# A hybrid decoder layer: gates in seven half-size products, token sums on VectorE, two buffers for streamed weights

## The chip, the cores and the metric

The kernel runs on one core of one Trainium2 chip. Its time is the device time of one execution in microseconds; the median of three runs is given. PE is TensorE, DVE is VectorE, ACT is ScalarE, POOL is GpSimd, and SP is SyncE, which issues nearly all DMAs.

## The reference, cut to what matters

One layer with 4096 tokens of width 1024. Three head groups read the same normalised input `h`; the gate path is a part of the combined projection, SiLU of which multiplies the groups before the output projection.

```python
shift, scale, gate = jnp.split(c_act @ ada_w + ada_b, 3, axis=-1)
h = _rmsnorm(x, g_pre) * (1.0 + scale[:, None]) + shift[:, None]
proj = h @ w_in
aq, ak, av, ag, rkv, rg, gq, gkk, gv, gg = jnp.split(proj, list(np.cumsum(IN_SPLITS)[:-1]), axis=-1)
attn = _sliding_window_attention(...)
attn = attn * jax.nn.silu(ag)
...
rwkv = rwkv * jax.nn.silu(rg)
gla = _gla_mixer(h, gq, gkk, gv, gk1, gk2, gk_b, gla_norm_w) * jax.nn.silu(gg)
y = jnp.concatenate([attn, rwkv, gla], axis=-1) @ w_out
return x + gate[:, None] * _rmsnorm(y, g_post)
```

The gates `ag`, `rg` and `gg` together are a 1024 x 1024 product with `h`, as wide as the output projection.

## The kernel before, in words

Work goes in 16 steps of 256 tokens, in two halves. The first half (the block from line 644 on) computes `h`, transposed, as an f16 pair of high and low parts (`hT`: channel, 2 parts, 8 channel blocks, 256 tokens), and the RWKV and linear-attention groups, whose results go to HBM (`mscr`), as `hT` does (`hscr`). Beside it `stage_c` splits the weights of the second half into scaled f16 pairs and writes them to HBM (`wscr`, `woscr`). The second half does the attention projections (`qkv`, `heads_of`), the gates (`gates`, `gates_of`), the banded attention (`stage_s`, `attend`), the gating (`stage_m`) and the output projection with its norm (`outp`).

A product of two f16 pairs takes three matmuls (high by high, high by low, low by high). The gates are four column groups of 256 (`Wq[3]` to `Wq[6]`); `proj` makes each as two halves of 8 x 3 matmuls of 256 tokens, into one PSUM bank `gp`; ACT takes its tanh and DVE closes it (`ag`). The output projection is already in seven half-size products (Strassen's scheme in Winograd's form): `stage_m` builds sums of the gated blocks, `block` splits them into pairs (`mtp`), `outp` runs products `PRODUCTS`, each 12 matmuls of 512 columns into a bank `op`, and DVE adds the banks into `yv`. Four of its seven weight sets stay in SBUF (`o1`, `o6`, `o4`, `o5`), three are loaded anew in each step, in halves, into one buffer `ov`.

What sets the order: each engine's order is fixed beforehand by a planner, `Order.pin` (line 220), which simulates costs of its own and takes, of what is ready, the lowest rank: the place in the program less `order.urgent`. `URGENT` (line 36) lifts what frees a bank. Streams of stages (`streams`, `emit`) set the place in the program; `stage_p2` (line 1991) strings gates, projections and output of neighbouring steps together.

In the linear attention a 128 x 256 state `Gst` with a block-diagonal mask `bdm` is kept by one 128 x 256 f32 matmul `kvp` and three DVE operations per 128 tokens (`stage_r`, lines 1409 to 1417). Softmax rows are scaled by DVE (line 1756).

Of the kernel before, what the change touches and what calls it, by code (L numbers as in the profile page):

```python
# [35 lines left out]
URGENT = 150  # L36
# [362 lines left out]
def hybrid_kernel(ctx, tc, x, rows, ada1, adaw, w1, wl, w2, wo, cst, abias, out):  # L399
# [51 lines left out]
    wscr = dp.tile([7, P, 2, KD * 256], F16, name="wscr")  # L451
# [192 lines left out]
    with ExitStack() as p1:  # L644
# [233 lines left out]
        def wo_squares(h):  # L878

            for j in range(16 * h, 16 * h + 16):  # L880
                s32 = wt([P, 256], "cs", 2)
                SP.dma_start(s32, wo[:, j * 256 : (j + 1) * 256])
                yield [s32]
                S.activation(wt([P, 2, 256], "ch", 2, F16)[:, 0], s32, AF.Square, accum_out=wo_ss[:, j : j + 1])
            if h == 0:
                return
            sst = st.tile([P, 1], F32, tag="wss", name="wss")
            V.tensor_reduce(sst, wo_ss, axis=AX.X, op=ALU.add)
# [5 lines left out]
            pow2(wo_sc, w_inv[7], tot)  # L894

        def wo_group(k, c):


            left, right = [wt([P, 256], "cs", 2) for _ in range(2)]
            for t, k8 in ((left, k), (right, 4 + k)):  # L900
                for h in range(2):
                    col = c * P + h * 512
                    at = (col // 256) * 2048 + k8 * 256 + col % 256
                    SP.dma_start(t[:, h * P : (h + 1) * P], wo[:, at : at + P])
            w11, w12, w21, w22 = left[:, 0:P], left[:, P:], right[:, 0:P], right[:, P:]
            yield [left, right]

            def parts(t, p):
                m = t.shape[-1] // P
                t = t.rearrange("p (m c) -> p m c", m=m)  # L910
                z = wt([P, 2, 2, P], "ch", 2, F16)[:, 0:m]
                S.activation(z[:, :, 0, :], t, AF.Identity, scale=wo_sc)
                V.scalar_tensor_tensor(z[:, :, 1, :], t, wo_sc, z[:, :, 0, :], op0=ALU.mult, op1=ALU.subtract)
                SP.dma_start(woscr[p : p + m, :, k, c].rearrange("m p h c -> p m (h c)"), z.rearrange("p m h c -> p m (h c)"))

            parts(w11, 0)
            parts(right, 1)
# [3 lines left out]
            parts(left, 3)  # L921
# [3 lines left out]
            parts(right, 5)  # L925

        def stage_c(i):

            yield [("c", i - 1), ("vg", i)]
            for n in ((0,), (1, 2), (3,), (4, 5), (6,))[i] if i < 5 else ():  # L930
                src = w2[:, n * 2048 : (n + 1) * 2048]
                inv = w_inv[n]


                def piece(j):
                    s32 = wt([P, 256], "cs", 2)
                    SP.dma_start(s32, src[:, j * 256 : (j + 1) * 256])
                    return s32

                ss = st.tile([P, 2, KD], F32, tag="wss8", name="wss8")  # L940
                for j in range(KD):
                    s32 = piece(j)
                    yield [s32]
                    S.activation(wt([P, 2, 256], "ch", 2, F16)[:, 0], s32, AF.Square, accum_out=ss[:, 0, j : j + 1])
                    if n == 2:
                        S.activation(wt([P, 2, 256], "ch", 2, F16)[:, 0][:, 0:P], s32[:, 0:P], AF.Square, accum_out=ss[:, 1, j : j + 1])
# [3 lines left out]
                for o, iv, sx in parts:  # L950
                    sst = st.tile([P, 1], F32, tag="wss", name="wss")
                    V.tensor_reduce(sst, ss[:, o, :], axis=AX.X, op=ALU.add)
                    yield [sst, "mq"]
                    sp = mq("wssp")
                    PE.matmul(sp[:, 0:1], ones, sst, start=True, stop=True)
                    tot = st.tile([P, 1], F32, tag="wtot", name="wtot")
                    V.tensor_copy(tot, sp[:, 0:1])
                    pow2(sc if sx is None else sx, iv, tot)
                for j in range(KD):
                    s32 = piece(j)  # L960
                    yield [s32]
                    hi, lo = [t[:, n] for t in (wt([P, 2, 256], "ch", 2, F16),) for n in range(2)]
                    S.activation(hi, s32, AF.Identity, scale=sc)
                    V.scalar_tensor_tensor(lo, s32, sc, hi, op0=ALU.mult, op1=ALU.subtract)
                    SP.dma_start(wscr[n, :, 0, j * 256 : (j + 1) * 256], hi)
                    SP.dma_start(wscr[n, :, 1, j * 256 : (j + 1) * 256], lo)
# [12 lines left out]
                if n > 2:  # L979
                    V.tensor_single_scalar(g_h[n - 3], inv, 0.5, op=ALU.mult)  # L980
            if 4 <= i < 6:
                yield from wo_squares(i - 4)
            elif 6 <= i < NS - 2:
                for g in (i - 6, i + 2):
                    yield from wo_group(g % 4, g // 4)
# [392 lines left out]
        def stage_r(i):  # L1378
# [30 lines left out]
            for a in range(2):  # L1409
                gidx = 2 * i + a  # L1410
                Gc, Gn = Gst[gidx % 2], Gst[(gidx + 1) % 2]
# [17 lines left out]
                yield [Gn, "mq"]  # L1429
# [135 lines left out]
    def pool2(name):  # L1565
# [3 lines left out]
        "q", "kT", "vt", "w5", "w6", "ab", "v4", "pr", "mxa", "ag", "mtp", "mxb", "sm1", "o1", "o6", "o4", "o5", "ov")}  # L1569
# [8 lines left out]
    Wq = []  # L1578
# [48 lines left out]
    def qkv(i):  # L1627
# [12 lines left out]
        yield from heads_of(hT, q, kT, vt_, pjt, mq if i > 1 else pjt)  # L1640
# [592 lines left out]
```

## Time and profile before

| | us |
|---|---|
| median of 3 runs (2060.5 to 2067.3) | 2060.84 |
| the profiled execution's own time | 2064.53 |
| its span | 2062.4 |
| PE busy in the span | 1952.8 (95%) |
| DVE busy | 1608.5 (78%) |
| ACT busy | 1154.2 (56%) |
| POOL busy | 215.2 (10%) |

The span is from the first to the last instruction. Busy time counts an instruction from its start to its end; a matmul's end is modelled and overlaps the next, so two starts, not two durations, give its pace. A row names engine, operation, output and inputs; nearly all rows have line 334, that of the helper that records every operation, so they are told apart by the names of tiles.

### The profile page before, as it was taken

The numbers are of one execution on the slowest core, as the hardware profiler recorded it, in microseconds if no ns is written. First come the engines' busy times: TensorE is split into PE (matmuls) and PEld (weight loads), VectorE is DVE, ScalarE is ACT, GpSimd is POOL, SyncE is SP. The second block draws the span as 40 slices with busy tenths as digits, with TensorE's granted clock in tenths as the row PEclk, the third lists the DMA queues.
The fourth block names the chain that finished last, engine by engine and source line by source line (L and its number), as shares of the span: only waits on it lengthen the run. The fifth ranks groups of instructions, "written<-read, shape, count | busy, mean of one in ns | idle before, by whom it ended". The sixth has DMA issues, their size and how long they took to land.

```text
span 2062.4 us, 61554 instructions
## 1 busy us (share of the span) xinstructions
PE 1952.8 (95%) x24931; PEld 1515.7 (73%) x24931; DVE 1608.5 (78%) x5211; ACT 1154.2 (56%) x2765; POOL 215.2 (10%) x405
## 2 busy tenths in 40 slices
PE   5899999999999999999898999999999999999997
PEld 2678777787787877777777677777787777877783
DVE  5787888878877688996767887877778877778877
ACT  5867776576776856766334544443444444444543
POOL 1511111521111111111100000000000000000000
PEclk8999999999999999999999999999999999999999
DMA  9332233323322413345323434343334333333315
GB/s 366 109 100 75 80 102 105 87 92 110 92 88 82 129 37 98 114 128 181 108 73 134 162 108 144 117 134 100 124 114 147 106 126 116 115 124 130 123 45 175
DMA packets 182504, 242.11 MB, mean 117 GB/s; under 512 B 51650, under 2 KB 140226, under 8 KB 177988
## 3 DMA queue, kind: packets, MB, share of 16 engines
q1 hardware_dynamic: 182068, 237.57, 35.6%
q8 instruction: 198, 3.24, 0.7%
q14 instruction: 94, 0.77, 0.1%
q10 hardware_dynamic: 144, 0.52, 0.1%
HBM read 177.20 MB, written 60.82 MB: 115 GB/s over the span
## 4 chain that ended last, share of the span: by engine, by line
PE 57%; DVE 24%; DMA 8%; ACT 6%; issue 3%; SPq 2%; POOL 0%; DVEq 0%; ACTq 0%; POOLq 0%
PE gp L334 16%; PE op L334 12%; PE zz L334 5%; PE qp L334 3%; PE lp L334 3%; SPq L334 2%; PE sc L334 2%; DVE mtp L334 2%; PE ovp L334 2%; DVE q L334 2%; PE kp L334 2%; DVE pr L334 2%; PE gqk L334 2%; DMA cs<-in_wo 1%; DVE ch L334 1%
## 5 line engine op out<-in xcount | busy, mean ns | idle before, releaser
L334 PEld LDWEIGHTS <-mtp 128*128 128x128 f16 x1344 | 130.3, 98 | 141.0 <-issue 3.2
L334 PE MATMUL op<-o,mtp 128*128 128x512 f16 x768 | 172.3, 379 | 0.0
L334 ACT ACTIVATE pr<-pr,nm,lsc 128x256 f32<-128x256 f32 (+1 forms) x256 | 149.3, 585 | 33.8 <-DVE nm L334 33.7
L334 PE MATMUL op<-ov,mtp 128*128 128x512 f16 x576 | 143.1, 379 | 0.5 <-DVE q L334 0.5
L334 PEld LDWEIGHTS <-hT 128*128 128x128 f16 x1536 | 117.5, 99 | 26.0 <-issue 3.9
L334 DVE CUSTOM_DVE_ANT_0 pr<-sc,ab,kept 128x256 f32<-128x256 f32 (+1 forms) x256 | 108.6, 475 | 10.6 <-PE sc L334 10.4
L334 DVE TENSOR_TENSOR yv<-op,yv 128x512 f32<-128x512 f32 x105 | 70.3, 680 | 47.8 <-PE op L334 33.7
L334 PE MATMUL pv<-gvh,hT 128*128 128x272 f16 x512 | 98.8, 283 | 7.3 <-DVE kg L334 3.0
L334 ACT ACTIVATE ag<-gp,gh 128x512 f32<-128x512 f32 x64 | 43.7, 683 | 109.5 <-PE gp L334 109.5
L334 POOL COPY kT<-kT 128x512 f16<-128x512 f16 x15 | 10.1, 676 | 844.4 <-DVE kT L334 815.3
L334 ACT ACTIVATE mtp<-yv,oi 128x1024 f16<-128x1024 f32 x30 | 34.3, 1143 | 111.7 <-DVE yv L334 111.3
L334 PE MATMUL lp<-hT,Lh 128*128 128x256 f16 x512 | 93.5, 276 | 0.1
L334 DVE SCALAR_TENSOR_TENSOR ag<-ag,gp 128x512 f32<-128x512 f32 x64 | 43.7, 683 | 59.7 <-ACT ag L334 59.7
L334 PE MATMUL zz<-hT,vh 128*128 128x256 f16 x512 | 88.8, 273 | 1.3 <-DVE zb L334 1.3
L334 PE MATMUL zz<-hT,rh 128*128 128x256 f16 x512 | 89.9, 275 | 0.0
L334 PE MATMUL zz<-hT,kh 128*128 128x256 f16 x512 | 89.8, 273 | 0.0
L334 PE MATMUL gqk<-hT,gqkh 128*128 128x256 f16 x512 | 89.8, 276 | 0.0
L334 PE MATMUL gp<-hT,q5h 128*128 128x256 f16 x512 | 87.0, 273 | 1.4 <-DVE ag L334 1.4
L334 PE MATMUL gp<-hT,q3h 128*128 128x256 f16 x512 | 86.0, 273 | 1.9 <-DVE yv L334 1.4
L334 PE MATMUL qp<-hT,q1h 128*128 128x256 f16 x512 | 86.0, 273 | 0.6 <-DVE kT L334 0.6
L334 PE MATMUL qp<-hT,q0h 128*128 128x256 f16 x512 | 85.2, 273 | 1.1 <-DVE nwt L334 1.1
L334 PE MATMUL gp<-hT,q6h 128*128 128x256 f16 x512 | 85.5, 273 | 0.0
(460 smaller groups left out, 6034.9 us busy)
## 6 DMA issues: line engine op xcount, KB each, us to landing
ov<-woscr SPq DMA_DIRECT2D x96, 512.0 KB, 3.8
xt<-in_x SPq DMA_DIRECT2D x16, 1024.0 KB, 5.1
hscr<-hT SPq DMA_DIRECT2D x16, 1024.0 KB, 5.3
hT<-hscr SPq DMA_DIRECT2D x16, 1024.0 KB, 5.2
x<-in_x SPq DMA_DIRECT2D x30, 512.0 KB, 4.2
out<-yv SPq DMA_DIRECT2D x30, 512.0 KB, 2.9
cs<-in_w SPq DMA_DIRECT2D x112, 128.0 KB, 2.4
v<-vscr SPq DMA_DIRECT2D x128, 64.0 KB, 2.3
```

The source lines that it names most:

```text
L334: r = f(*args, **kw)
```

## The change

The gates become seven half-size products, too. `h` is cut in four quarters (128 tokens by 512 channels), `sums` builds four combinations of them on DVE, with ACT's casts for their high parts (`sg`, in step 0 `mtp`), and a product runs 4 x 4 x 3 matmuls of 128 tokens; DVE and ACT combine the banks into `ag`. The weights are combined in the first half (`group`, for gates and output alike, in pieces of 512 columns) and lie in `gwscr`. Four of seven gate sets stay in SBUF (`g`). Gates and output share two buffers for streamed sets (`ov`, `ov2`), which `feed` fills two sets ahead, in halves; of the output's sets one more (5) is streamed. Sets 0 of the last gates and the last two outputs have room of their own.

Besides: `heads_of` takes the gates between keys and values, and values go before the queries; the scaling of softmax rows goes to ACT; the reciprocal root of single columns needs fewer operations; `URGENT` is 600 and covers the blocks and their scale; the linear-attention state is kept packed, 128 x 64.

```diff
-URGENT = 150
+URGENT = 600
...
+        if n == 1:
+            for c in (3.0, 12.0, 768.0):
+                V.scalar_tensor_tensor(tt[:, :n], y, y, v, op0=ALU.mult, op1=ALU.mult)
+                V.scalar_tensor_tensor(y, tt[:, :n], -c, y, op0=ALU.add, op1=ALU.mult)
+            V.tensor_single_scalar(y, y, -1.0 / 8192, op=ALU.mult)
+            return
...
-                if gidx > 0:
-                    V.tensor_scalar(Gc, Gc, egm[:, a, 0:1], None, op0=ALU.mult)
+                V.scalar_tensor_tensor(heads4[0], now.rearrange("p (o n) -> p o n", o=1).to_broadcast([P, 4, HD]),
+                                       egm[:, a, 0:1], heads4[1], op0=ALU.mult, op1=ALU.mult)
                 kvp = mq("kvp")
-                PE.matmul(kvp[:, :NT], kt[:, a, :], vg[:, a, 0:256], start=True, stop=True)
-                V.tensor_tensor(Gn, kvp[:, :NT], Gc, op=ALU.add)
-                V.scalar_tensor_tensor(Gn, Gn, egp[:, a, 128:129], bdm, op0=ALU.mult, op1=ALU.mult)
+                joint()
+                for h in range(4):
+                    PE.matmul(kvp[32 * h : 32 * h + 32, 0:HD], kt[:, a, 32 * h : 32 * h + 32], vg[:, a, h * HD : h * HD + HD],
+                              start=True, stop=True)
+                joint(False)
+                V.scalar_tensor_tensor(then, now, egm[:, a, 0:1], kvp[:, 0:HD], op0=ALU.mult, op1=ALU.add)
+                V.tensor_scalar(then, then, egp[:, a, 128:129], None, op0=ALU.mult)
...
+    PRODUCTS = ((0, False), (1, True), (6, True), (3, False), (4, True), (5, False), (2, False))
+    GATES = ((1, True), (0, False), (6, True), (4, False), (3, True), (5, True), (2, False))
...
+    def feed(h):
+
+        if fed[h] < len(feeds):
+            src, n = feeds[fed[h]]
+            SP.dma_start(Wv[fed[h] % 2][:, 2 * h : 2 * h + 2], src[n, :, 2 * h : 2 * h + 2])
+            fed[h] += 1
...
+        whole(X, 1, 0)
+        whole(Y, 1, 1)
+        later()
+        V.tensor_tensor(Y, X, Y, op=ALU.add)
+        parts(Y, 0)
+        whole(Z, 0, 0)
+        later()
+        V.tensor_tensor(Y, Y, Z, op=ALU.subtract)
+        parts(Y, 1)
+        later()
+        V.tensor_tensor(X, Z, X, op=ALU.subtract)
+        parts(X, 2)
+        whole(Z, 0, 1)
+        later()
+        V.tensor_tensor(Z, Z, Y, op=ALU.subtract)
+        parts(Z, 3)
...
+        moving = (a12, a11, s2, s3, s1, a22, s4)
...
+            for c in range(4):
+                for k in range(KD // 2):
+                    for a, b in ((0, 0), (0, 1), (1, 0)):
+                        PE.matmul(po[:, c], W[c // 2][:, c % 2, k, a, :], moving[n][b][:, k, :],
+                                  start=k == a == b == 0, stop=k == KD // 2 - 1 and a == 1)
+                    if c % 2 and k == KD // 2 - 1 and not stays and W is not own:
+                        after(c // 2)
...
+        def close(to, j, z, t):
+            for m in range(2):
+                S.activation(t[:, 2 * m : 2 * m + 2], z[:, 2 * m : 2 * m + 2], AF.Tanh, scale=g_h[2 * j + m])
+            V.scalar_tensor_tensor(to, t, 1.0, z, op0=ALU.add, op1=ALU.mult)
...
+        yield from full(0)
+        soon(S.copy, Y, banks[0])
+        yield from full(1)
+        soon(V.tensor_tensor, g11, banks[1], Y, op=ALU.add)
+        soon(S.copy, X, banks[1])
+        yield from full(2)
+        soon(V.tensor_tensor, g12, banks[2], X, op=ALU.add)
+        close(g11, 0, g11, Y)
+        yield from full(3)
+        soon(V.tensor_tensor, g22, banks[3], g12, op=ALU.add)
+        yield from full(4)
+        soon(S.copy, X, banks[4])
+        V.tensor_tensor(g12, g12, X, op=ALU.add)
+        V.tensor_tensor(Z, g22, X, op=ALU.add)
+        yield from full(5)
+        soon(V.tensor_tensor, g21, banks[5], g22, op=ALU.add)
+        close(g22, 1, Z, X)
+        close(g21, 0, g21, Y)
+        yield from full(6)
+        soon(V.tensor_tensor, g12, banks[6], g12, op=ALU.add)
+        close(g12, 1, g12, Z)
...
-            V.tensor_scalar(pr[h // 4][:, h % 4, k0:], pr[h // 4][:, h % 4, k0:], rd[:, h : h + 1], None, op0=ALU.mult)
+            S.activation(pr[h // 4][:, h % 4, k0:], pr[h // 4][:, h % 4, k0:], AF.Identity, scale=rd[:, h : h + 1])
...
+        elif 1 < i < NS - 1:
+            if i < NS - 2:
+                yield from outp(i - 1)
+            yield from stage_u(i)
+            yield from qkv(i + 1, gates(i))
```

In `sums`, `whole` adds the two parts of a quarter on DVE, and `parts` casts a sum on ACT and subtracts on DVE.

The planner's order moves in three places. On PE, at the border of two gate products in the middle of the second half (`q3` and `q4` are column groups of the weights before, `g` and `ov` weight sets now, h and l their parts), before:

```order
L334 LDWEIGHTS q4h
L334 MATMUL gp<-hT,q4h 128x256
L334 LDWEIGHTS q4l
L334 MATMUL gp<-hT,q4l 128x256
L334 LDWEIGHTS q4h
```

and in the change:

```order
L334 MATMUL gp<-hT,g_18592 128x128
L334 LDWEIGHTS ov
L334 MATMUL gp<-hT,ov 128x128
L334 MATMUL ovp<-pr,v_21067 64x128 x14
L334 MATMUL ovp<-pr,v_22070 64x128 x2
```

A gate matmul has half the tokens, and every one still comes with a weight load of its own; products on streamed weights (`ov`) stand between those on weights that stay.

On DVE, where the scale of the gated values (`mtot` to `msc`) leads to the first block of the output product (`mtp`), before:

```order
L334 TENSOR_REDUCE mtot<-mp 128x1
L334 TENSOR_SCALAR p2e<-mtot 128x1
L334 TENSOR_SCALAR p2e<-p2e 128x1 x2
L334 TENSOR_SCALAR p2f<-p2e 128x1
L334 TENSOR_SCALAR p2e<-p2e 128x1
L334 TENSOR_SCALAR msc<-p2f 128x1
L334 TENSOR_SCALAR miv<-p2e 128x1
L334 TENSOR_TENSOR oi<-miv,winv_98 128x1
L334 SCALAR_TENSOR_TENSOR mtp<-mxa,msc,mtp 128x512
```

and in the change (`xg` and `sg` are the token sums, `q` the queries):

```order
L334 TENSOR_REDUCE mtot<-mp 128x1
L334 TENSOR_TENSOR xg_18559<-xg_18561,xg_18559 128x512
L334 TENSOR_SCALAR p2e<-mtot 128x1
L334 TENSOR_TENSOR xg_18561<-hT 128x512
L334 TENSOR_SCALAR p2e<-p2e 128x1
L334 TENSOR_TENSOR sg_18555<-xg_18560,sg_18555 128x512
L334 SCALAR_TENSOR_TENSOR q<-qp,q 64x512
L334 TENSOR_SCALAR p2e<-p2e 128x1
L334 TENSOR_TENSOR sg_18556<-xg_18559,sg_18556 128x512
L334 SCALAR_TENSOR_TENSOR q<-qp,q 64x512
L334 TENSOR_SCALAR p2f<-p2e 128x1
L334 TENSOR_SCALAR p2e<-p2e 128x1
```

One more sum (`xg`) follows before `msc`; what stood in a row is now drawn apart by five sums and two operations on the queries.

On SP, the DMAs of a step of the second half from the next tokens (`hT`) on (`vscr` and `v` spread the values, `mxb` the first half's results), before:

```order
L334 DMA hT<-hscr 128x4096
L334 DMA vscr<-vt 128x2x128
L334 DMA ov<-woscr 128x2048
L334 DMA v_24516<-vscr 32x4x128 x4
L334 DMA v_24517<-vscr 32x4x128 x4
L334 DMA ov<-woscr 128x2048 x3
L334 DMA mxb<-mscr 128x1024
L334 DMA ov<-woscr 128x2048 x2
L334 DMA out<-yv 128x1024
```

and in the change:

```order
L334 DMA hT<-hscr 128x4096
L334 DMA ov<-woscr 128x2048 x2
L334 DMA vscr<-vt 128x2x128
L334 DMA v_25082<-vscr 32x4x128 x4
L334 DMA v_25083<-vscr 32x4x128 x4
L334 DMA ov_18553<-woscr 128x2048 x2
L334 DMA mxb<-mscr 128x1024
L334 DMA ov<-woscr 128x2048 x2
L334 DMA ov_18553<-gwscr 128x2048 x2
L334 DMA ov<-gwscr 128x2048 x2
L334 DMA ov_18553<-gwscr 128x2048 x2
L334 DMA out<-yv 128x1024
```

Between the next tokens and the output six sets now stand, where three stood; they come from two places and go to two buffers in turn, one set of them ahead of the values.

## Rows read from the trace of the kernel before

**Rows 1.** Stages (windows): us, busy of PE, PEld, DVE, ACT, POOL, PE clock, DMA share, GB/s.

```profile
400.00:500.00 100.00, 97.80 (x1429) 79.46 (x1427) 79.82 (x320) 74.44 (x177) 17.26 (x38) 1.00 0.38 114
...
1000.00:1120.00 120.00, 103.08 (x1633) 82.86 (x1631) 79.39 (x295) 48.06 (x124) 8.18 (x15) 0.96 0.29 91
...
1364.46:1426.95 62.49, 61.60 (x639) 46.89 (x638) 48.89 (x136) 27.97 (x71) 0.61 (x1) 1.00 0.37 121
```

**Rows 2.** Page part 4, the chain that ended last, shares by engine.

```profile
PE 57%; DVE 24%; DMA 8%; ACT 6%; issue 3%; SPq 2%; POOL 0%; DVEq 0%; ACTq 0%; POOLq 0%
```

**Rows 3.** Timeline of PE in one step: start, duration (us), idle before.

```profile
1373.37 5.34 PE L334 MATMUL op<-o,mtp 128*128 128x512 f16 x24
...
1415.41 0.28 PE L334 MATMUL mp<-mss,first 128*128 128x2 f32 x2
...
1422.70 1.89 PE L334 MATMUL op<-ov,mtp 128*128 128x512 f16 x8
...
1425.48 0.60 PE L334 MATMUL sc<-kT,q 128*128 128x256 f16 x4 [0.89 <-DVE m L334]
```

**Rows 4.** Costliest groups of that step, PE: busy us, mean ns, idle before.

```profile
L334 PE MATMUL gp<-hT,q5h 128*128 128x256 f16 x32 | 5.5, 273 | 0.0
...
L334 PE MATMUL gp<-hT,q4l 128*128 128x256 f16 x16 | 4.4, 273 | 0.0
```

**Rows 5.** Timeline of PE, the 48 matmuls of one gate's column group.

```profile
1201.29 0.38 PE L334 MATMUL gp<-hT,q4h 128*128 128x256 f16 x2
...
1206.53 0.38 PE L334 MATMUL gp<-hT,q5h 128*128 128x256 f16 x2
```

**Rows 6.** Timeline of PE's weight loads, the value projection.

```profile
1481.53 2.77 PEld L334 LDWEIGHTS <-hT 128*128 128x128 f16 x48
...
1484.26 0.81 PEld L334 LDWEIGHTS <-q 128*128 128x128 f16 x8
```

**Rows 7.** Groups of that step, DVE.

```profile
L334 DVE TENSOR_TENSOR yv<-op,yv 128x512 f32<-128x512 f32 x7 | 4.7, 680 | 3.4 <-PE op L334 2.3 <-issue 1.2
...
L334 DVE TENSOR_SCALAR pr<-pr,rd 128x256 f32<-128x256 f32 x16 | 4.5, 348 | 0.1
...
L334 DVE SCALAR_TENSOR_TENSOR q<-qp,q 64x512 f16<-64x512 f32 x4 | 2.8, 688 | 1.9 <-ACT q L334 1.9
...
L334 DVE SCALAR_TENSOR_TENSOR ag<-ag,gp 128x512 f32<-128x512 f32 x4 | 2.7, 686 | 4.4 <-ACT ag L334 4.4
```

**Rows 8.** Timeline of DVE in that step.

```profile
1376.26 1.25 DVE L334 TENSOR_TENSOR yv<-op,yv 128x512 f32<-128x512 f32 x2
...
1377.43 1.22 DVE L334 STREAM_TRANSPOSE pr<-pr 128x1024 f32<-128x1024 f32 x1
...
1416.66 0.16 DVE L334 TENSOR_REDUCE mtot<-mp 128x1 f32<-128x2 f32 x1
...
1418.67 0.75 DVE L334 SCALAR_TENSOR_TENSOR mtp<-mxa,msc,mtp 128x512 f16<-128x512 f32 x1 [0.53 <-ACT mtp L334]
```

**Rows 9.** Groups of that step, ACT.

```profile
L334 ACT ACTIVATE vt<-vp,winv 128x256 f32<-128x256 f32 x1 | 0.5, 473 | 0.0
```

**Rows 10.** DMA of that step: GB/s in slices, packets, issues (KB each, us to landing).

```profile
GB/s 198 143 321 5 0 52 281 278 60 10 194 170 296 178 189 58 320 294 0 0 10 0 0 160 286 226 0 147 393 142 0 0 0 0 0 10 0 0 110 316
...
DMA packets 3144, 7.57 MB, mean 121 GB/s; under 512 B 337, under 2 KB 1598, under 8 KB 3009
...
ov<-woscr SPq DMA_DIRECT2D x6, 512.0 KB, 3.8
```

**Rows 11.** Timeline of PE, the linear-attention state in the first half.

```profile
113.27 0.60 PE L334 MATMUL kvp<-vg,kt 128*128 128x256 f32 x2
...
113.80 0.65 PE L334 MATMUL op<-Gst,qg 128*64 128x256 f32 x4
```

**Rows 12.** Groups of the whole span by form, DVE, splits of output weights.

```profile
L334 DVE SCALAR_TENSOR_TENSOR ch<-cs,wsc,ch 128x256 f16<-128x256 f32 x56 | 29.8, 539 | 6.5 <-ACT ch L334 5.9 <-DMA adr<-AT 0.3
```

**Rows 13.** Page part 5, costliest groups, weight loads of tokens.

```profile
L334 PEld LDWEIGHTS <-hT 128*128 128x128 f16 x1536 | 117.5, 99 | 26.0 <-issue 3.9
```

More of the change, by code (lines that the diff above doesn't have):

```diff
@@ L900, in wo_group, with group @@
+        def group(gate, k, c):
+            src, base, sc = (w2, 3, g_sc[c]) if gate else (wo, 0, wo_sc)
+            left, right = [wt([P, 512], "cs", 2).rearrange("p (h n) -> p h n", h=2) for _ in range(2)]
             for t, k8 in ((left, k), (right, 4 + k)):
                 for h in range(2):
[L902 to L905, printed above, removed]
+                    at = (base + c + 2 * h) * 2048 + k8 * 256
+                    SP.dma_start(t[:, h], src[:, at : at + 256])
+            w11, w12, w21, w22 = left[:, 0], left[:, 1], right[:, 0], right[:, 1]
@@ L918, in wo_group @@
+            if gate:
+                for t in (w12, w22):
+                    V.tensor_scalar(t, t, g_r[c], None, op0=ALU.mult)
+            parts(w11, 0, 1)
+            parts(right, 1, 2)
             V.tensor_tensor(w11, w12, w11, op=ALU.subtract)
@@ L950, in stage_c @@
                 for o, iv, sx in parts:
[L951 to L960, printed above, removed]
-                    yield [s32]
[L962 to L966, printed above, removed]
+                    yield from total(ss[:, o, :], sc if sx is None else sx, iv)
+                for j in range(4):
+                    s32 = piece(w2, n * 2048 + j * 512)
+                    yield [s32]
+                    z = split_tile().rearrange("p c h n -> p (c h n)").rearrange("p (h n) -> p h n", h=2)
+                    S.activation(z[:, 0], s32, AF.Identity, scale=sc)
+                    V.scalar_tensor_tensor(z[:, 1], s32, sc, z[:, 0], op0=ALU.mult, op1=ALU.subtract)
+                    SP.dma_start(wscr[n, :, :, j * 512 : (j + 1) * 512], z)
                 if n == 2:
@@ L978, in stage_c @@
                 V.tensor_scalar(inv, inv, hinv, None, op0=ALU.mult)
[L979 to L985, printed above, removed]
+            if 3 <= i < 5:
+                for n in (i, i + 2):
+                    yield from gate_squares(n)
+            elif 5 <= i < 7:
+                yield from wo_squares(i - 5)
+            for _ in range((0, 0, 0, 0, 1, 1, 1, 2, 2, 2, 2, 2, 2, 1, 0, 0)[i]):
+                yield from group(*next(groups))
         def stage_g(_):
@@ L1658, in heads_of @@
         model.order.urgent = 0
+        if mid is not None:
+            yield from mid
+        yield ["pj"]
+        vp = pj("vp")
+        for a in range(2):
+            yield from proj_tok(vp[:, a * P : (a + 1) * P], Wq[2], P, P, hT, a * P)
+        model.order.urgent = URGENT
+        S.activation(vt_.rearrange("p a n -> p (a n)"), vp[:, :NT], AF.Identity, scale=Wq[2][2])
+        model.order.urgent = 0
+        spread()
         for n in range(2):
-            yield ["pj"]
-            qp = pj("qp")
+            yield ["m" if n and pv is mq else "pj"]
+            qp = mt("qp") if n and pv is mq else pj("qp")
             for b in range(2):
@@ L1670, in heads_of @@
             model.order.urgent = 0
-        yield ["mq" if pv is mq else "pj"]
-        vp = pv("vp")
-        for a in range(2):
-            yield from proj_tok(vp[:, a * P : (a + 1) * P], Wq[2], P, P, hT, a * P)
-        model.order.urgent = URGENT
-        S.activation(vt_.rearrange("p a n -> p (a n)"), vp[:, :NT], AF.Identity, scale=Wq[2][2])
-        model.order.urgent = 0
     def spread_values(vt_, v4, i):
@@ L1686, in gates, with stage_u @@
+    def stage_u(i):
+        load_h(i)
+        yield [F[i]["hT"]]
+        F[i]["S"] = blocks if i == 0 else sums_t
+        sums(F[i]["hT"], F[i]["S"])
     def gates(i):
-        yield [("og", i - 2)]
+        yield [("og", i - 1)] if i > 1 else []
         f = F[i]
-        f["ag"] = ag = t_A([P, 8, NT], "ag") if i == 0 else pools["ag"].tile([P, 8, NT], F32, name="ag2") if i == 1 else F[i - 2]["ag"]
-        yield from gates_of(f["hT"], ag, pjt)
+        f["ag"] = t_A([P, 8, NT], "ag") if i < 2 else F[1]["ag"]
+        yield from gates_of(f["hT"], f["S"], f["ag"], feed, own=Wx.get(("g", i)))
@@ L1714, in stage_s, with home, attend @@
         vblk = [F[i - 1]["v"][1] if i > 0 else None, *v4]
[L1715 removed]
+        def home():
+            if "mx" not in f:
+                f["mx"] = wt([P, 4, NT], "mxa", 2)
+            return f["mx"]
         for a in range(2):
[L1717 to L1719 removed]
+            yield from attend(q, kT, vblk, home, a, i == 0 and a == 0, sct=sct, ovt=ovt, gate=[("o", i - 2)])
+    def attend(q, kT, vblk, home, a, first, before=None, sct=("at", "sq"), ovt=("tr", "m", "y", "mq"), gate=()):
         k0 = P if first else 0
@@ L2031, in hybrid_kernel @@
     xo, gn = x2[:, 0, :], x2[:, 1, :]
-    mtp = pools["mtp"].tile([P, 4, 2, 4, P], F16, name="mtp")
-    blocks, split = [mtp[:, n] for n in range(4)], []
     streams((0, "v", stage_v, None), *((1, "s", stage_s, i) for i in range(1, NS)), *((2, "m", stage_m, i) for i in range(NS)),
```

283 lines of the change are left out of this document (184 added, 99 removed).

## The prediction

> **What bounds the kernel now.** I read the stages first, then the chain of waits, then the groups of one step. The stage view gives two neighbouring parts of the second half and one of the first [rows 1]: a 256-token step takes 62.49 us, in which PE is busy 61.60, DVE 48.89 and ACT 27.97; the granted clock is 1.00, the upper of its two levels. The chain that ended last lies on PE for 57% of the span and on DVE for 24% [rows 2]; with PE at 61.60 of 62.49, a step of the second half ends when PE has worked through its matmuls. Of its waits one is worth a name: 0.89 us for a score bank that DVE frees [rows 3]. In the first half PE is busy 97.80 of 100 us and DVE 79.82; where the halves meet, PE idles 17 us of 120 [rows 1]. So two questions decide: what the gates cost PE after the change, and whether DVE, which pays for them, still hides.
>
> **Gates on PE.** A step's gates are now 4 x (32 + 16) = 192 matmuls of 256 columns [rows 4]. 48 of them start over 1206.53 - 1201.29 = 5.24 us [rows 5], 0.1092 us each, 20.97 us a step. The change makes 7 products x 4 x 4 x 3 = 336 matmuls of 128 columns, each still with its own weight load. The same shape is in the trace: the value projection's 48 loads, one before each 128-column matmul, take 1484.26 - 1481.53 = 2.73 us [rows 6], 0.0569 us each. So 336 x 0.0569 = 19.12, and 1.85 us a step come back; 16 x 1.85 = 29.6 us. Seven products for eight would give 2.6 a step, but half as wide a matmul costs 0.52, not 0.50, of a full one. Break-even is 20.97 / 336 = 0.0624 us a matmul.
>
> Here a page speaks against the change. The Trainium skill, "TensorE: Matmul & The Clock Gate", section "Back-to-back issue gap", says that in real streams of load and matmul a 128-column matmul takes about 81 ns, a 512-column one about 131. By that the new gates would cost 336 x 0.081 = 27.2 us a step and the kernel would lose some 100 us. This trace agrees with neither figure: 57 ns for the first, and 24 of the second take 5.34 us [rows 3], over 216 each. I keep the row.
>
> **VectorE.** Removed a step: 16 scalings of the softmax, 4.5 us [rows 7], which go to ACT, and four tiny steps of the shorter root, at the 0.16 of such a row [rows 8] 0.6 us. The four closing multiplies of a gate stay four. Added: 12 operations of 512 columns for the token sums (of hi and lo halves into f32, their combinations, the new low halves) and 7 that combine products. One costs 0.585 where two follow each other (1377.43 - 1376.26, [rows 8]) and 0.680 as a group [rows 7]; 19 make 11.1 to 13.0. Net +6.0 to +7.9: DVE is busy 54.9 to 56.8 of about 61 us, 90 to 93%. It hides behind PE as long as it fills the waits that it has today, where its next instruction waits for ACT or PE: 4.4 us before the gates' multiplies, 3.4 before the output sums, 1.9 before q [rows 7]. The sums are ranked below everything, and the order puts them between other operations.
>
> That has a price at one place, the second order excerpt. The step's scale goes through seven small DVE operations, and the first output product waits for it. Now mp starts at 1415.41 and the product at 1422.70 [rows 3], 7.29 us later; the scale's first operation starts at 1416.66 and the block is done at 1418.67 + 0.75 = 1419.42 [rows 8], 3.3 us early. In the change five sums stand between those seven, 5 x 0.585 = 2.9, and on PE 54 or 60 projection matmuls and 8 score matmuls follow mp, 6.8 to 7.4 us at 0.1092. The block comes at 4.0 + 2.9 = 6.9: between 0.5 early and 0.1 late, with nothing left for a wait on ACT in the two q rows between. Bounds: 0, and 1.0 (a q row with its share of the 1.9 wait). I take 0.4 a step, 6.4 us in all, nearer to the lower end, since only some of the chain's waits can fall there. Behind the block nothing else is late: the next ones have a product of 2.6 us each.
>
> **ScalarE.** 16 scalings at the 0.473 of a 256-column row [rows 9], four casts for the new hi halves and three bank copies at twice that, and eight tanh halves of 256 columns add at most 7.6 + 6.6 + 3.8 = 18.0: 46 of 61 us. Cost nothing; if DVE waits for it, that is the 0.4 above.
>
> **Weights and SP's queue.** Streamed sets go from 3 to 7 a step, 6 to 14 halves of 512 KB [rows 10]. The step moves 7.57 + 4.2 = 11.8 MB, 193 GB/s over 61 us; single slices of today's step show 393 [rows 10]. With two buffers the shortest return is one buffer's: out product 5 to gate product 0, with out product 2 and gate product 1 between, 2.6 + 2.7 = 5.3 us, and as much again as half a product, 1.3, for each half. A half lands in 3.8 us. Today's shortest, out 3 to out 2, is 5.2 and shows no wait worth naming. The third excerpt shows what is queued: the scattered v loads and the next hT stand behind loads that wait for PE, as before. Cost nothing; if the cover goes, see the rivals.
>
> **The first half.** The linear-attention state becomes a quarter as wide. Its kvp matmul holds PE for 113.80 - 113.27 = 0.53 us [rows 11], 32 times, 17 us. The new one, four of 32 x 64 side by side, saves at most all of that and at worst nothing; two changes of the array's tiling are against it, and PE is not free to use all of it. I take a quarter, 4 us. DVE's three state operations get narrower. The preparation of the weights handles 512 columns at a time, and gates are split in seven parts like the output weights: where 56 splits of 0.539 us [rows 12] stood, 12 and 32 wider ones stand with 32 more adds, about as much in all. DVE has 20 us of 100 free there, so it costs nothing; the bound is 8 us either way, about a third of what PE idles there at 2.2 us in 100 [rows 1]. Where the halves meet, 24 sums (14 us of DVE, which has 40 of 120 free) come before the first gates; again nothing, at half of PE's idle time, 8 us, either way. At the end the last gates save their 1.85 like the others, and the last output blocks are unchanged.
>
> **The sum.** -29.6 + 6.4 - 4 = -27.2. The profiled execution took 2064.53 us, 3.7 over the median of the three runs, 2060.84; it would take 2037.3, and the runs 2033.6. I forecast 2034. Its own range: late blocks 0 to 16, kvp 0 to -17, and twice 8 either way that hardly add up in full: 2016 to 2049.
>
> **Rivals.** *DVE sets the pace.* For it: 54.9 to 56.8 busy, and an in-order engine whose waits for ACT between two halves of a bank (kT and q) no order of work removes; the 13.6 us that it idles today would have to shrink to 4 to 6. If 6 us of its waits stay, a step takes 56.8 + 6 = 62.8, 0.3 over now; 16 x 0.3 - 4 gives +1, and with the sums filling part of them 0.2 to 0.5 less a step: about 2057. Against it: the sums depend only on hT, which is there a step earlier. 18%.
>
> *The weight stream is late*: the slower one. Place: the two returns of 5.2 and 5.3 us. In 5.2 us around out product 5 four halves, 2.1 MB, are asked for, 400 GB/s, above the highest slice of 393. A half has 6.5 us; up to there nothing is lost. At a landing of 9 us each return is 2.5 late, 5.0 a step, 14 steps 70 us, less 27: 2104. It decides from about 7.2 us on, where two returns cost the 1.45 that a step gains. Against it: 3.8 us today, at 37% of the DMA engines' time in a step [rows 1]. 7%.
>
> *The narrow matmul does not keep 0.0569.* A weight load by itself takes 99 ns [rows 13]. If in the gates it no longer ran beside the matmul before it, 336 x 0.099 = 33.3 us, +12.3 a step: about 2260. The Trainium skill's 81 ns, named above, is the milder form of this. Against it stands the value projection, 48 loads in 2.73 us in the midst of the same step. 3%.
>
> **How the numbers follow.** The forecast's case has 72%. A measurement of this kernel tells 0.5% from no change, 10.3 us, so faster begins at 2050.5. Of the 72, 64 lie below that; of the first rival's 18, 3 are faster, 13 the same, 2 slower; the other 10 are slower. Faster 0.67, same 0.21, slower 0.12. The range takes the forecast's own and reaches up to the first rival: 2014 to 2059, which leaves out the last two rivals and the ends.
>
> **What would show it.** Right: a step of 60.5 to 61.5 us, gate matmuls of 128 columns starting every 57 ns, DVE at 90% or more in a step and not first on the chain, ACT near 40 us. The first out product after mp shows an idle of some tenths released by DVE mtp. Wrong: out or gp matmuls on ov that wait for a DMA (second rival); PE idle of over 1.5 us a step released by DVE at several places (first); a pitch over 62 ns in gp (third). The first half would be at odds with me if its end moved by over 10 us.

## The result, and the profile after

The change takes 2072.66 us (median of 20 runs, 2064.35 to 2076.13) where the kernel before takes 2065.59 (20 runs, among them the three ahead of the prediction, which had 2060.84). The ratio is 1.0036, 95% interval 1.0026 to 1.0046: 7.4 us slower, clear of noise but under the 0.5% that the prediction counts as a change, where 2034 was forecast. The profiled execution took 2073.81 us, its span 2072.0, 9.6 us over the span before.

First the stages again, now of the change, with columns as in [rows 1]: one stretch of the first half and two steps of the second.

```profile
400.00:500.00 100.00, 91.74 (x1465) 74.81 (x1464) 91.68 (x318) 68.68 (x150) 29.90 (x46) 0.97 0.37 111
...
1422.82:1486.16 63.34, 61.31 (x790) 47.52 (x789) 54.57 (x134) 39.62 (x98) 1.04 (x1) 1.00 0.55 186
1486.16:1548.75 62.59, 59.74 (x778) 46.12 (x776) 54.94 (x134) 39.60 (x98) 1.04 (x1) 1.00 0.56 188
```

A step takes 62.97 us on the mean of these two, 0.5 more than before. PE is busy 60.5 (1.1 less than before), so it now idles 2.4 us a step, not 0.9. DVE is busy 54.8, the lower end of the forecast. In the stretch of the first half that is shown PE falls from 97.80 to 91.74 where DVE rises from 79.82 to 91.68.

To see where the difference lies, both traces are split at the first scale, the start of the first `mtot`. It comes at 1117.35 us before and at 1127.02 in the change, 9.7 us later; what follows, before and then in the change, is equally long:

```profile
1117.35:2062.38 945.03, 918.02 (x9403) 688.76 (x9401) 742.73 (x2053) 425.17 (x1074) 11.41 (x15) 1.00 0.37 122
```

```profile
1127.02:2072.03 945.01, 897.47 (x11448) 684.82 (x11445) 821.21 (x2022) 592.34 (x1466) 15.90 (x15) 1.00 0.55 188
```

So behind the first scale the gates' gain and its price cancel, and in these two traces the loss lies ahead of it. (A stretch of one trace can be off by 7 to 9 us; see the last section.)

The chain that ended last (the page's part 4) has changed sides; [rows 2] had PE 57% and DVE 24%:

```profile
DVE 42%; PE 31%; ACT 11%; DMA 9%; issue 5%; SPq 2%; POOL 0%; DVEq 0%; ACTq 0%; POOLq 0%
```

PE's waits over eight steps of the change (1296.58 to 1801.45 us; what waited and for whom, then us in all, how often, the longest):

```profile
PE op L334 <- ACT mtp L334: 6.2, 7, 1.2
PE op L334 <- DVE mtp L334: 4.0, 12, 0.6
PE mp L334 <- DVE kT L334: 3.9, 8, 0.9
PE sc L334 <- DVE m L334: 3.8, 8, 0.6
PE kp L334 <- ACT mxa L334: 1.0, 3, 0.5
PE ovp L334 <- DVE pr L334: 0.3, 1, 0.3
```

Eight steps of the kernel before (1291.71 to 1791.54 us) had one line in this view:

```profile
PE sc L334 <- DVE m L334: 7.0, 8, 0.9
```

The new waits, 15.4 us of them, lie between the keys (`kT`), the scale and the first output blocks (`mtp`). On PE's timeline, with the gates' pace at its end:

```profile
1484.54 0.35 PE L334 MATMUL mp<-mss,first 128*128 128x2 f32 x2 [0.39 <-DVE kT L334]
...
1490.65 1.04 PE L334 MATMUL sc<-kT,q 128*128 128x256 f16 x8
1492.83 0.60 PE L334 MATMUL op<-ov,mtp 128*128 128x512 f16 x2 [1.15 <-ACT mtp L334]
...
1530.23 2.84 PE L334 MATMUL gp<-hT,g 128*128 128x128 f16 x48
1532.91 2.84 PE L334 MATMUL gp<-sg,ov 128*128 128x128 f16 x48
```

A gate product starts 2.68 us after the one before it, 0.0558 us a matmul; the forecast's 0.0569 holds, and seven take 18.8 us. What PE waits for is seen on DVE at the same place (start, duration):

```profile
1481.10 0.96 DVE L334 SCALAR_TENSOR_TENSOR kT<-kp,kq_s,kT 64x256 f16<-64x256 f32 x2
1482.09 0.69 DVE L334 TENSOR_TENSOR mxa<-mxa 128x512 f32<-128x512 f32 x1
1482.70 0.68 DVE L334 TENSOR_TENSOR xg<-hT 128x512 f32<-128x512 f16 x1
1483.40 0.99 DVE L334 SCALAR_TENSOR_TENSOR kT<-kp,kq_s,kT 64x256 f16<-64x256 f32 x2
1484.42 0.69 DVE L334 TENSOR_TENSOR sg<-xg,sg 128x512 f16<-128x512 f32 x1
1485.15 0.98 DVE L334 TENSOR_TENSOR xg<-xg,xg 128x512 f32<-128x512 f32 x1
1486.16 0.16 DVE L334 TENSOR_REDUCE mtot<-mp 128x1 f32<-128x2 f32 x1
...
1491.42 0.14 DVE L334 TENSOR_SCALAR msc<-p2f 128x1 int32<-128x1 int32 x1
```

and on ACT:

```profile
1491.54 0.62 ACT L334 CAST sg<-xg 128x512 f16<-128x512 f32 x1 [2.55 <-DVE xg L334]
1492.06 0.72 ACT L334 ACTIVATE mtp<-mxa,msc 128x512 f16<-128x512 f32 x1
```

DVE has no gap here. A token sum stands between the two pairs of `kT`, so `mp` is late. `mtot` then starts 1.62 us after `mp` (1.25 before, [rows 3, 8]), behind two more sums, and when the scale is there at 1491.42, ACT casts a sum first. Two halves of this step in the stage view show how uneven DVE's load is:

```profile
1473.70:1504.00 30.30, 27.95 (x287) 19.69 (x285) 29.33 (x62) 16.41 (x32) 1.04 (x1) 1.00 0.33 108
1504.00:1536.00 32.00, 31.60 (x483) 26.07 (x481) 25.36 (x75) 22.65 (x65) 0.00 (x0) 1.00 0.73 241
```

In the first 30 us DVE is busy 97% and PE idles 2.35 us, in the next 32 DVE is busy 79% and PE idles 0.40. The DMA rows of the streamed weights (page part 6: how often, KB, us to landing), to be held against [rows 10]:

```profile
ov<-woscr SPq DMA_DIRECT2D x124, 512.0 KB, 5.3
ov<-gwscr SPq DMA_DIRECT2D x94, 512.0 KB, 4.7
```

They land later than the 3.8 us of before, but no matmul waits for one. The residual `x` lands later too (5.5 us on the page, 4.2 before), and DVE, which had no wait for a DMA in the eight steps before, now waits for it some 7 us ahead of its full 30 us (one place, then eight steps):

```profile
1467.06 1.23 DVE L334 TENSOR_TENSOR yv<-yv,x 128x1024 f32<-128x1024 f32 x1 [1.90 <-DMA x<-in_x]
```

```profile
DVE yv L334 <- DMA x<-in_x: 11.0, 8, 2.9
```

### The profile page after: what moved, and what is told of

Its sections match the earlier page's. It is cut to its first block, busy times and chain, and to the rows that moved or that the text cites. A ratio compares the mean times of both kernels' runs of the same rounds, so it can differ in the third digit from the quotient of the medians.

```text
span 2072.0 us, 66785 instructions
## 1 busy us (share of the span) xinstructions
PE 1940.2 (94%) x27427; PEld 1518.8 (73%) x27427; DVE 1710.0 (83%) x5174; ACT 1321.4 (64%) x3057; POOL 226.5 (11%) x405
## 4 chain that ended last, share of the span: by engine, by line
DVE 42%; PE 31%; ACT 11%; DMA 9%; issue 5%; SPq 2%; POOL 0%; DVEq 0%; ACTq 0%; POOLq 0%
PE op L334 9%; DVE pr L334 5%; PE zz L334 4%; DVE xg L334 3%; PE gp L334 3%; DMA x<-in_x 3%; ACT pr L334 2%; DVE mtp L334 2%; DVE yv L334 2%; DVE ag L334 2%; SPq L334 2%; PE lp L334 2%; DVE q L334 2%; DVE sg L334 2%; DVE mxa L334 2%
## 5 line engine op out<-in xcount | busy, mean ns | idle before, releaser
L334 PE MATMUL op<-ov,mtp 128*128 128x512 f16 x744 | 176.5, 379 | 10.8 <-ACT mtp L334 8.4
L334 PEld LDWEIGHTS <-g 128*128 128x128 f16 x3072 | 176.1, 98 | 4.2 <-issue 0.8
L334 PE MATMUL op<-o,mtp 128*128 128x512 f16 x576 | 135.5, 379 | 7.4 <-DVE mtp L334 4.5
L334 PEld LDWEIGHTS <-ov 128*128 128x128 f16 x2256 | 130.3, 98 | 2.5 <-DVE q L334 1.0
L334 ACT ACTIVATE pr<-pr,rd 128x256 f32<-128x256 f32 (+1 forms) x256 | 105.9, 492 | 18.3 <-DVE rd L334 18.1
L334 POOL COPY kT<-kT 128x512 f16<-128x512 f16 x15 | 14.6, 977 | 865.6 <-DVE kT L334 783.1
L334 PE MATMUL gp<-hT,g 128*128 128x128 f16 x1536 | 91.8, 219 | 0.0
L334 DVE STREAM_TRANSPOSE pr<-pr 128x1024 f32<-128x1024 f32 (+1 forms) x70 | 78.8, 1131 | 10.0 <-ACT pr L334 9.2
L334 PE MATMUL gp<-sg,g 128*128 128x128 f16 x1440 | 85.6, 219 | 0.5 <-DVE ag L334 0.5
```

Source lines behind the costliest of these rows:

```text
L334: r = f(*args, **kw)
```

## The experiments

Kernels are the change with one edit, if not said otherwise, and ratios are to the kernel before. Differences between two of them are taken from the ratios, times 2065.6 us; by the intervals they are good to 3 to 5 us where both kernels have 7 runs or more, to some 6 where one has 4. "Eight steps" are those from the fourth scale to the twelfth.

**e1: without the token sums.**

```diff
-        F[i]["S"] = blocks if i == 0 else sums_t
-        sums(F[i]["hT"], F[i]["S"])
+        F[i]["S"] = None
...
-        s1, s2, s3, s4 = [[t[:, b] for b in range(2)] for t in S_of]
+        s1, s2, s3, s4 = a11, a12, a21, a22
```

> Leaves out the token sums: the gate products read the four quarters of h in their place, so DVE loses 12 operations of 512 columns a step (some 7.5 us) and ACT four casts; PE's matmuls, weights and DMAs stay. Theory A (DVE is late between the gates and the first output product, and PE waits there for kT, mtp and m): the step falls from 63.0 to 60.2 to 61.0 us, PE's waits in a step from 2.4 to under 1.2 us, the run to 2030 to 2045 (ratio 0.983 to 0.990). Theory B (the narrow matmuls or the streamed weights cost PE what the products saved): the step stays above 62.5 us, ratio 1.000 or more.

Measured: 2046.42 us, ratio 0.9923 (0.9894 to 0.9952). Eight steps by stage and PE's waits in them:

```profile
1285.02:1777.00 491.98, 481.15 (x6258) 376.22 (x6257) 388.69 (x976) 300.67 (x752) 8.81 (x8) 1.00 0.57 192
```

```profile
PE mp L334 <- ACT mtp L334: 4.0, 8, 0.5
PE sc L334 <- DVE m L334: 3.6, 16, 0.3
PE kp L334 <- ACT mxa L334: 2.5, 7, 0.4
```

A step takes 61.50 us (63.11 in the change over eight steps); PE's matmuls and its weights are the same. So theory B falls and A holds, somewhat short of its numbers: 0.0113 of the time, 23 us (some 6 either way), is the price of the sums (with their casts). The trace shows 22 us of it behind the first scale, which comes at 1119.95 us:

```profile
1119.95:2043.02 923.07, 890.72 (x11438) 686.56 (x11437) 734.56 (x1854) 563.81 (x1408) 16.67 (x15) 1.00 0.57 192
```

The 61.5 are 1.0 under the step before, not the 2 that PE's products save. PE is busy 60.1 us of it, 1.5 less than before, and idles 1.35 where it idled 0.9; why its busy time falls by no more is not shown.

**e2: softmax scaling back on DVE** (`V.tensor_scalar` in place of `S.activation` at the scaling).

> Softmax scaling back on DVE: DVE gains 16 operations of 0.35 us (4.5 us busy) a step, ACT loses 16. Theory A (DVE is what is late): the step rises by 1 to 3 us, to 64 to 66 us, the run to 2090 to 2125 (ratio 1.010 to 1.028). Theory C (ACT is what is late: its scaling holds the transposes, and its casts stand ahead of mtp): the step does not rise, 62 to 63 us, ratio 0.995 to 1.004.

Measured: 2097.85 us, ratio 1.0155 (1.0119 to 1.0190), 64.2 us a step, 1.1 over the change, with DVE busy 58.0 us of it where the change has 54.7. DVE's work is what counts, as theory A has it; C falls.

**e3: the linear-attention state as before** (lines 1409 to 1417 put back).

> Only the linear-attention state as before (one 128 x 256 matmul, three wide DVE operations). Theory A (the packed state saves PE a little, as the prediction took it): the first half ends 0 to 6 us later, ratio 1.004 to 1.007. Theory D (the four small matmuls and their change of tiling cost more than they save): the first half ends 4 to 10 us sooner, ratio 0.999 to 1.002.

Measured: 2069.67 us, ratio 1.0033 (1.0014 to 1.0051), no difference from the change. The packed `kvp` takes 0.25 us of PE where the old one takes 0.53, so PE gains 9 us of time in the first half, and none of it is seen in the total: neither A nor D. Nor does it cost time that the wide operations keep DVE busy 14.6 us longer up to the first scale (e11).

**e4: the residual added on POOL** (`G.tensor_tensor` for `V.tensor_add` in `norm`).

> The residual is added on POOL (idle in the second half) in place of DVE: DVE loses two operations of 1.23 us a step and its wait for the residual's DMA (1.25 us a step). Theory A: the step falls by 1 to 2 us, to 61 to 62 us, the run to 2040 to 2058 (ratio 0.989 to 0.997). Theory E (DVE's own time is not what counts, only the order around the scale; or POOL and DVE hinder each other): 62.7 to 63.5 us, ratio 1.002 to 1.006.

Measured: 2090.56 us, ratio 1.0131 (1.0104 to 1.0157), 64.2 us a step: worse than both theories. DVE has two operations of 1.22 us less in a step, yet is busy 440.6 us in eight steps where the change has 437.9. POOL's timeline in one step, then DVE's:

```profile
1469.58 2.36 POOL L334 TENSOR_TENSOR yv<-yv,x 128x1024 f32<-128x1024 f32 x1 [40.25 <-DVE yv L334]
1479.68 2.35 POOL L334 TENSOR_TENSOR yv<-yv,x 128x1024 f32<-128x1024 f32 x1 [7.74 <-DMA x<-in_x]
```

```profile
1470.22 1.73 DVE L334 TENSOR_TENSOR ry<-ry,oi 128x1 f32<-128x1 f32 x1
...
1480.06 2.53 DVE L334 TENSOR_TENSOR ag<-ag,xg 128x512 f32<-128x512 f32 x1 [0.57 <-ACT xg L334]
```

A DVE operation on one column lasts 1.73 us, to the end of POOL's add at 1471.94, and one on 512 columns 2.53 us, to just behind the end of the next; in the change `ry<-ry,oi` takes 0.154 on the mean, `ag<-ag,xg` 0.686 (in e4 0.546 and 1.152). Both have two inputs from SBUF, and both stand still while POOL adds. The Trainium skill says it so too: in "SBUF — State Buffer", section "SBUF: two separate sides", the port pair that DVE and GpSimd share is a lock held for a whole instruction, and whoever comes second is blocked. The trace agrees, with 1.73 and 2.53 us.

**e5: most token sums held until the scale is there.**

```diff
-        whole(Z, 0, 0)
+        if after is None:
+            whole(Z, 0, 0)
+        else:
+            one = st.tile([P, 1], F32, tag="one", name="one")
+            later()
+            V.tensor_scalar(one, after, 0.0, 1.0, op0=ALU.mult, op1=ALU.add)
+            later()
+            V.scalar_tensor_tensor(Z, quarter(hT, 0, 0, 0), one, quarter(hT, 1, 0, 0), op0=ALU.mult, op1=ALU.add)
...
-        sums(F[i]["hT"], F[i]["S"])
+        sums(F[i]["hT"], F[i]["S"], F[i - 1].get("msc") if i > 1 else None)
```

(`after` is the scale `msc` of the step ahead. The edit holds eight sums of twelve, from the fifth on, not nine.)

> Nine of the twelve token sums (from the fourth on) wait for the step's scale msc, by a column of ones made from it: one tiny DVE operation more a step, all else as in the change; the sums move from between kT, mtot and msc to behind the first output blocks. Theory A1 (it is the place of the sums that costs, since DVE is full between the gates and the first output product and has some 5 us a step of waits later): the step falls to 61.3 to 62.2 us, PE's waits for mp and the first op go, the run to 2045 to 2060 (ratio 0.990 to 0.997). Theory A2 (it is their amount: DVE is late wherever they stand): 62.8 to 63.5 us, ratio 1.002 to 1.006, with waits of gp or sc in place of mp and op.

Measured: 2063.79 us, ratio 0.9991 (0.9980 to 1.0001). PE's waits in eight steps:

```profile
PE sc L334 <- DVE m L334: 7.0, 9, 0.9
PE kp L334 <- ACT mxa L334: 5.2, 8, 1.7
PE mp L334 <- ACT mtp L334: 3.9, 8, 0.5
```

The waits of the output products and of `mp` for `kT` are gone, steps settle at 61.95 us, and 9 us of the run come back with DVE's work unchanged (436.2 us in eight steps, 437.9 in the change). A1 holds for the steps; the run falls short of it, and behind the first scale the trace is 5.9 us shorter (939.15, 945.01). DVE's wait for the residual shrinks as well, from 11.0 to 1.6 us, so the place of the sums is not told apart from that wait (e6). The stretch from the 14th scale to the end grew from 144.0 to 149.0 us, since the last gates now wait for a scale (e9).

**e6: the planner is told later landings** (in its costs `(512, 5.5)` for `(512, 3.5)`, and 5.5 for 4.8 above 512 KB).

> The planner is told 5.5 us for a DMA of 512 KB (3.5 before; the trace of the change shows 5.3 and 4.7 to landing), so it sets the second residual add of a step behind other DVE work. Theory X (DVE's 1.25 us a step of waiting for the residual x, just ahead of its full stretch, is what makes it late): the wait goes and the step falls by 0.7 to 1.3 us, the run to 2050 to 2062 (ratio 0.992 to 0.998). Theory A2: the wait goes but the step stays at 62.7 to 63.5 us, ratio 1.002 to 1.006.

Measured: 2079.51 us, ratio 1.0077 (1.0053 to 1.0102). DVE's waits for the residual fall from 11.0 to 4.9 us in eight steps and a step to 62.8, but the first scale comes at 1137 us, 10 later than in the change: the edit moved the order of the first half too. It does not tell X from A2.

**e7: `URGENT = 150`.**

> URGENT 150 in place of 600, everything else as in the change. Theory A: the scale and the blocks come later still, the step rises by 0 to 1 us, ratio 1.003 to 1.012. Theory U (600 pushes urgent work ahead of softmax and so makes m late): the step falls by 0.3 to 1 us, ratio 0.996 to 1.002.

Measured: 2104.41 us, ratio 1.0186 (1.0162 to 1.0209), 65.3 us a step, far beyond theory A's 1.012; U falls. Steps alternate between 62.2 and 68 us, and one line leads the waits:

```profile
PE gp L334 <- ACT xg L334: 17.7, 4, 4.4
```

With the lower rank a gate product waits up to 4.4 us for its bank's copy. So the higher rank is a part that the change needs.

**e8: e5 with the old state** (the edits of e3 and e5).

> The held sums with the old linear-attention state. If both effects are real and add: first half 5 to 9 us sooner than with the held sums alone, ratio lower by 0.002 to 0.004 than that run's. If the first half's end only moves the idle time to the transition: the same ratio as the held sums alone, within 0.001.

Measured: 2064.11 us, ratio 0.9993 (0.9980 to 1.0005): as e5. With e3 this bounds the state's worth to under some 3 us either way.

**e9: e5, but not in the last two steps** (`if 1 < i < NS - 2`).

> The held sums, but not in the last two steps, whose gates come ahead of the output that they would wait for (with sums held there too the stretch from the 14th scale to the end took 149.1 us, in the change 144.0). Theory A1: steps stay at 61.9 to 62.1 us, the end is 4 to 6 us sooner than with all sums held, the run at 2056 to 2062 (ratio 0.995 to 0.998). If the tail was longer for another reason: ratio 0.998 to 1.000 as before.

Measured: 2059.85 us, ratio 0.9982 (0.9967 to 0.9996); from the 14th scale to the end 146.1 us. The end comes back by 2.9 us of the 5 where 4 to 6 were expected; the ratio lies 2 us under e5's, within noise, and between the two theories. Behind the first scale the trace is as long as e5's (939.13 us), since one step takes 65.1.

**e10: e9 with the combined weights prepared a step later.**

```diff
-            for _ in range((0, 0, 0, 0, 1, 1, 1, 2, 2, 2, 2, 2, 2, 1, 0, 0)[i]):
+            for _ in range((0, 0, 0, 0, 0, 1, 1, 1, 2, 2, 2, 2, 2, 2, 1, 0)[i]):
```

> The same, with the combined weights prepared one step later in the first half (steps 5 to 14 in place of 4 to 13), off the stretch from 400 to 700 us, where DVE is 84 to 92 percent busy and PE idles 7 to 8 us in 100. Theory P (the preparation crowds DVE there and delays the first half): the first half ends 3 to 10 us sooner, ratio 0.991 to 0.996. Theory O (the first half's end moves with its order by some us for no one cause): it ends within 5 us either way, and the ratio within 0.002 of the run beside it.

Measured: 2054.11 us, ratio 0.9954 (0.9938 to 0.9970), the fastest of the kernels that leave nothing out and faster than both. The step from e9 is 0.0028, 6 us, and the two intervals just overlap. But the first half ends no sooner in the trace: the first scale comes at 1117.86 us, e9's at 1117.72. The gain lies behind it (931.79 us, 939.13 in e9), where both kernels have the same order on DVE and ACT. So this is not theory P, and whether and why e10 is faster than e9 stays open.

**e11: the change without the sums of the gates' weights** (the two scalings and four subtractions of `group` for output weights only).

> The change without the sums that combine the gates' weights: 4 subtractions and 2 scalings for each of 8 pieces are left out, so the gates' weights are plain pieces; splits, DMAs and PE's work stay. DVE loses some 20 us of the first half. Theory P: the first half ends 5 to 12 us sooner, ratio 0.997 to 1.001. Theory O: it ends within 4 us, ratio 1.001 to 1.006.

Measured: 2057.36 us, ratio 0.9966 (0.9953 to 0.9979), 0.0070 or 14.5 us less than the change. The first scale comes at 1104.06 us, not 1127.02, in a profiled run that was the fastest of its ten. Stages from 400 to 700 us, of the kernel before:

```profile
400.00:700.00 300.00, 289.53 (x4468) 235.56 (x4466) 234.03 (x868) 212.77 (x506) 48.66 (x100) 0.99 0.32 97
```

of the change:

```profile
400.00:700.00 300.00, 276.67 (x4338) 224.25 (x4337) 267.69 (x917) 209.50 (x439) 62.81 (x109) 0.99 0.38 114
```

of e11, then of e3:

```profile
400.00:700.00 300.00, 290.25 (x4767) 238.06 (x4765) 271.22 (x931) 216.63 (x458) 78.17 (x120) 1.00 0.36 112
```

```profile
400.00:700.00 300.00, 283.67 (x4305) 229.49 (x4303) 273.73 (x927) 213.46 (x445) 66.10 (x115) 0.99 0.38 114
```

In the change DVE is full there (89%, 78% before) and PE idles 23 us in 300, where it had idled 10. Without the weight sums DVE is as full, but PE gets through 4767 matmuls, 429 more. That is theory P's direction, beyond its numbers. That the amount of DVE's work is the cause is not shown, for e3 speaks against it. Up to the first scale, in the change, e3 and e11:

```profile
0.00:1127.02 1127.02, 1042.69 (x15983) 834.00 (x15984) 888.81 (x3154) 729.04 (x1593) 210.62 (x390) 0.98 0.38 119
```

```profile
0.00:1120.30 1120.30, 1042.18 (x15791) 838.04 (x15792) 903.43 (x3152) 731.73 (x1593) 210.55 (x392) 0.98 0.38 120
```

```profile
0.00:1104.06 1104.06, 1032.31 (x15983) 831.56 (x15984) 874.35 (x3105) 729.28 (x1593) 220.43 (x390) 0.98 0.38 122
```

e11 takes 14.5 us off DVE and gains as much; e3 puts 14.6 us on DVE, spread over all steps, and loses nothing. Both edits also change the planner's order. Whether the weights' sums cost by their amount, by their place or by the order that comes with them stays open.

**e12: e10 with the subtractions of the weights on POOL** (`G.tensor_tensor` for `V.tensor_tensor` in `group`). **e13: e10 one step later still** (`0, 0, 0, 0, 0, 0, 1, 1, 2, 2, 2, 2, 2, 2, 2, 0`).

> The kernel of the late preparation, with the four subtractions of 256 columns a piece (64 in all, 0.44 us each on DVE) on POOL, which is 18 percent busy in the first half. Theory P (the amount of DVE work in the preparation delays the first half): DVE loses 28 us, the first half ends 6 to 15 us sooner, ratio 0.988 to 0.993. Theory E (POOL and DVE hinder each other, as the residual add on POOL suggests): DVE's other operations grow by about as much, the first half ends within 5 us, ratio 0.993 to 0.999.

> The kernel of the late preparation, one step later still for the first two pieces (steps 6 to 14). Theory P: if the stretch from 400 to 700 us is still what DVE crowds, the first half ends another 1 to 4 us sooner, ratio 0.993 to 0.996; Theory O: within 3 us either way and a ratio of 0.994 to 0.998.

Measured: e12 2059.31 us, ratio 0.9978 (0.9964 to 0.9993), 0.0024 over e10 with intervals that overlap. DVE loses 12 us of busy time up to the first scale (892.6 to 880.6), not 28: theory E, as in e4. e13 2057.72 us, ratio 0.9961 (0.9947 to 0.9976), as e10. Both later placings (0.9954, 0.9961) lie below e9's 0.9982, by some 5 us. But e13's first scale comes at 1127.16 us, 9.4 later than e9's, and its gain, like e10's, lies behind it (932.55 us). So the two do not show that the place of the weights' preparation delays the first half.

## Why the prediction was wrong

**Gates on PE: the pace right, the gain less.** 18.8 us a step stand where 20.97 stood, some 2 saved as forecast (1.85), with 0.0558 us a matmul against 0.0569. The Trainium skill's 81 ns ("TensorE: Matmul & The Clock Gate", "Back-to-back issue gap") does not hold here; the row did. The third rival falls, and so does the second as far as PE goes: the weights land in 4.7 to 5.3 us and no matmul waits. "Cost nothing" is still not whole for the DMAs, since DVE's 1.4 us a step of waiting for the residual are new. And the -29.6 did not arrive: with no sums in the way (e1) the stretch behind the first scale falls by 22 us.

**VectorE: the amount right, the price wrong.** DVE's 54.8 us lie at the lower end of 54.9 to 56.8. The first step that failed is "0.4 a step, 6.4 us in all": e1 measures the sums at 23 us, 1.6 a step. I had priced the one place that the order excerpt showed, the seven small operations of the scale, and put the block between 0.5 early and 0.1 late. On the chip the lateness begins ahead of that place: DVE comes to it already behind, `mp` itself waits for `kT`, and after the scale ACT's cast of a sum stands ahead of `mtp`. What I left out is that the slack of [rows 7] lies elsewhere in the step: DVE's largest wait in eight steps of the change is 29.5 us for output products, where no sum was put. By e5 and e9, 9 to 11 us come back at equal work when most sums stand there (6 us of them behind the first scale in the traces). How the rest of the 23 divides, no run tells.

**The first half: wrong.** "About as much in all" is near for the amount: in the groups from 100 to 1100 us DVE's splits, adds and scalings of these weights take 86.4 us where 79.5 stood. The second step that failed is what was drawn from it, "so it costs nothing; the bound is 8 us either way". The first scale comes 9.7 us later, and e11 gives 14.5 us back without the sums of the gates' weights. The 20 us of free DVE time in 100 was a mean: from 400 to 700 us DVE fills up to 89%, and PE idles 23 us. What in the sums costs this stays open (e3, e10, e13). The "4 us" for the packed state came to nothing (e3, e8): PE's 0.28 us for each of 32 products is saved, but PE was not what the first half waited for.

**The sum.** -29.6 for the gates, +23.3 for the sums, +14.5 for the weights' preparation and 0 for the state make +8.2, near the measured +7.4; but that is in part luck. No run shows the -29.6, and a part of e1's 23.3 may lie ahead of the first scale, where its trace is 7 us sooner. By stretch, from one trace each, the account is plainer: behind the first scale -22 and +22 cancel, and the loss lies ahead of it. Two terms failed: the sums were priced at little over a quarter of what they cost, and the preparation of the weights at nothing.

**The rivals.** "DVE sets the pace" is what came, with the sign that I had named for it: PE idles 2.4 us a step, over the 1.5, released by DVE and ACT at several places. But it came by another way than I wrote: not by 56.8 us of work plus waits that no order removes, but by 30 us of a step in which DVE is busy 97%, with its waits left over at other places. Its 0.3 us a step over before, less 0.2 to 0.5 for waits that the sums fill, became 0.5 to 0.6. In hindsight 18% was too low: DVE already stood on 24% of the chain that ended last [rows 2].

## What to carry to other kernels

An engine's busy share over a step does not tell its slack at a given place (here 87% of a step, but 97% of 30 us in it): before work is added to a second engine, look for where in the step its waits lie, and price the work at the stretch in which it will be put. Work that fills gaps by rank was put here into the first gap that the planner believed in; if what it feeds is needed much later, try holding it by a dependency until the urgent chain has passed (9 to 11 us here, at equal work). e10, which does that and prepares the weights a step later, is 0.46% under the kernel before.

## What had not been expected

POOL is no free hand for DVE: each add of 1024 columns on it (2.36 us) held up DVE operations with two inputs from SBUF to its end, so that 2.4 us less work a step on DVE left its busy time where it was and cost 20 us. And one program's stretches vary: the change, e4, e5 and e9 have the same program up to the first scale, yet it comes at 1127.02, 1126.70, 1125.32 and 1117.72 us. Behind it e9, e10 and e13 have the same order on DVE and ACT, and take 939.13, 931.79 and 932.55 us. The cause is open; a shift of under 10 us of a stretch in one profile, as in e3, tells nothing by itself, and the 9.7 us between the kernel before and the change lie just within that.
